# One inference step of a two-layer hybrid encoder: GpSimd's instructions in written order, weight additions issued a tile later

## The chip, the cores and the metric

The kernel runs on one core of a Trainium2 chip. TensorE multiplies, VectorE, ScalarE and GpSimd work on vectors, and DMA engines move data between HBM and the on-chip memory; a DMA is started by an instruction in the stream of SyncE (SP) or of GpSimd. The metric is the time of one launch on the device in microseconds (us). A row of the profile calls TensorE PE, VectorE DVE, ScalarE ACT and GpSimd POOL.

## The reference

There are 640 tokens (512 of a prompt, 128 of eight running streams), 1024 wide, and two layers, all in float32. The first is a Mamba-2 mixer, the second a gated MLP with position mixing (gMLP).

```python
# layer 0 (Mamba-2)
proj = rms_norm(h) @ w_in                      # -> z | x | B | C | dt
x, B, C = silu(causal_dwconv(xBC, conv_prev))  # width 4
# 32 heads in 8 groups; per chunk: decay, C B^T, states
h_new = h * exp(last) + einsum(B, w_in, x)
y = y + d_skip * x
y = gated_group_rms_norm(y, z, norm_w)
h = h + y @ w_out
# layer 1 (gMLP)
u, v, z = gelu(.), layer_norm(gelu(.)), .      # of rms_norm(h) @ w_in
h = h + (u * (W_s v + b) * silu(z)) @ w_out
y = rms_norm(h)
```

## The kernel before, in words

A float32 product is made of three products of rounded parts: an operand is split into a high part H (rounded) and a low part L (the rest), and HH, LH and HL are added up in PSUM.

**The first layer** goes through eight groups of heads, `g = 0` to `7`. A group multiplies the normed input by tiles of the input weights, 128 output columns each, by `in_proj`: x0, x1, B, C, z0 and z1. Each of x0, x1, B, C goes through `conv_tile`: VectorE scales it into `xp` (L407 to L409), ScalarE makes the first tap (`acc`, L414), VectorE adds three taps (L417), ScalarE takes a tanh (L423), VectorE ends it (`xc`, L424); TensorE then transposes `xc` into `tp` (L464). GpSimd clears three columns of `xp`, copies the cache into it and copies the new cache out of it (L405, L406, L411, L412). `pair(i)` makes the outputs of two heads from the decay matrices `E`, which `mask(i)` has multiplied by `CBm`: for `i = 0` on VectorE; for `i = 1` one `E` is masked on VectorE and one on GpSimd (both on GpSimd in the last group). `old_states` has GpSimd multiply eight slices of the old state `h0` by their decay (L582). `out_proj` multiplies the gated output of the group before by two tiles of output weights in ten pieces.

In groups 1 to 6 the written order between z0 and z1 is: `Wo = [stream.next(), stream.next()]`, `some(0, 1)`, `old_states` and other pieces, `some(1, 2)`, `some(2, 5)`, `mask(0)`, `pair(0)`, `mask(1)`, `some(5, 10)`, `pair(1)`, `gate(0)`, then z1 (a further `stream.next()`). `some(a, b)` are pieces a to b-1 of `out_proj` with `Wo`.

**Weights of the first layer** come through `Stream`, one unit for each tile. A unit has a tile `wh` and a tile `wl`; there are four buffers of each. For each unit `wsplit` writes three steps: GpSimd starts a DMA of the weights into `wh`, rounded on the way (L97); ScalarE writes their negative into `wl` (L98); GpSimd starts a second DMA of the same weights that adds into `wl` (L99). `next()` asks for units up to three behind the one that it returns, so the last unit asked for takes the buffer of the one used before the returned one. The list of units ends with sixteen of `wBv`; the second layer fetches `wBv` by itself (`v_fetch`, `v_split`, L808 to L816) and takes none of these from the stream.

**Order.** In the first layer only TensorE's instructions run as written. For every other engine a planner sets the order before the launch: it goes through a model of the time and gives an engine what is ready there. Each engine then runs its own list strictly in that order, and an instruction that waits holds up everything behind it on its engine. In the second layer all engines run as written.

**The second layer** splits its weights without GpSimd: `Forms.split` has ScalarE round a half tile (L743) and VectorE take the rest (L744). `forms.next(a)` returns a form and sees to it that `a` more behind it are split. `prod` asks for five ahead. `out_weights()` takes four forms by `forms.next(3)`; ten `out_piece` follow, each ended by a sum on VectorE (`accB`, L960).

Of the kernel before, what the change touches and what calls it, by code (L numbers as in the profile page):

```python
# [8 lines left out]
F32 = mybir.dt.float32  # L9
F32R = mybir.dt.float32r  # L10
I32 = mybir.dt.int32
AF = mybir.ActivationFunctionType
ALU = mybir.AluOpType
PSUM = bass.MemoryType.PSUM

P = 128
# [24 lines left out]
def hybrid_step(ctx: ExitStack, tc: tile.TileContext, xin, xT0, cst, wdt, cache, wA, wAo, h0in, wB, wBv, wBo,  # L41
                lnwb, spc, bsp, nwb, y_out, nconv_out, sspP_out, sspS_out, v_out):
    nc = tc.nc
    V, S, G, T = nc.vector, nc.scalar, nc.gpsimd, nc.tensor
# [46 lines left out]

    def wsplit(src):
        H = wpool.tile([P, 1024], F32R, name="wh", tag="wh", bufs=4)
        L = wpool.tile([P, 1024], F32R, name="wl", tag="wl", bufs=4)
        G.dma_start(out=H, in_=src)  # L97
        S.activation(L, H.bitcast(F32), AF.Identity, scale=-1.0)  # L98
        G.dma_start(out=L, in_=src, accum_op=ALU.add)  # L99
        return H, L  # L100

    class Stream:
        def __init__(self, srcs, ahead):
            self.srcs, self.ahead, self.got, self.n = srcs, ahead, [], 0

        def fill(self, ahead):
            while len(self.got) < min(len(self.srcs), self.n + ahead):
                i = len(self.got)
                self.got.append(wsplit(*self.srcs[i]))


        def first(self, n, between):
# [12 lines left out]

        def next(self, ahead=None):
            self.fill(1 + (self.ahead if ahead is None else ahead))
            r = self.got[self.n]
            self.got[self.n] = None
            self.n += 1  # L130
            return r
# [8 lines left out]
    def norm_first(zp, rb):  # L140
# [12 lines left out]
        for k in range(KD):  # L153
            w = C("nw0")[:, k:k + 1]
            S.activation(xH[:, k, :], xt[:, k, :], AF.Identity, scale=w)
            V.scalar_tensor_tensor(xL[:, k, :], xt[:, k, :], w, xH[:, k, :].bitcast(F32), ALU.mult, ALU.subtract)
        stream.fill(1)
        warm = ps_op.tile([P, 512], F32, name="warm", tag="op")
        for _ in range(13):
            mm(warm[:, :P], ones, ones)  # L160
# [148 lines left out]
        names += [p[0] for p in part]  # L309
        units += [p[1:] for p in part]  # L310
    units += wo(GROUPS - 2) + wo(GROUPS - 1)
    units += [(wBv[i],) for i in range(16)]
    stream = Stream(units, 3)


    with ExitStack() as ca:
# [9 lines left out]
        ptds = []  # L326
        side.append(lambda: ptds.append(norm_fin()))
        side += [lambda h=h: norm_half(*h) for h in HALVES]
        px1 = in_proj(stream.next(), xT, ps_op, "op", at=(2, 10, 12))
        ptd = ptds[0]  # L330
        nc.sync.dma_start(out=csb[1], in_=cst[:, NCST1:])

# [69 lines left out]
        def conv_tile(o0, o1, ft, j, cch, nconv):  # L402
            xp = w1.tile([P, 667], F32, name="xp", tag="xp")
            xps = xp[:, 515:667].rearrange("p (b j) -> p b j", j=19)
            G.memset(xp[:, 0:3], 0.0)  # L405
            G.tensor_copy(out=xps[:, :, 0:3], in_=cch[:, j])  # L406
            V.tensor_tensor(out=xp[:, 3:387], in0=o0, in1=rb[:, 0:384], op=ALU.mult)  # L407
            V.tensor_tensor(out=xp[:, 387:515], in0=o1[:, 0:128], in1=rb[:, 384:512], op=ALU.mult)
            V.tensor_tensor(out=xps[:, :, 3:19], in0=o1[:, 128:256].rearrange("p (b j) -> p b j", j=16),  # L409
                            in1=rb[:, 512:640].rearrange("p (b j) -> p b j", j=16), op=ALU.mult)  # L410
            G.tensor_copy(out=nconv[:, j, 0, :], in_=xp[:, 512:515])  # L411
            G.tensor_copy(out=nconv[:, j, 1:9, :], in_=xps[:, :, 16:19])  # L412
            acc = w1.tile([P, 667], F32, name="acc", tag="acc")
            S.activation(acc[:, 0:664], xp[:, 0:664], AF.Identity, scale=cw[:, 4 * ft:4 * ft + 1],  # L414
                         bias=cw[:, 128 + ft:129 + ft])
            for k in range(1, 4):
                V.scalar_tensor_tensor(acc[:, 0:664], xp[:, k:k + 664], cw[:, 4 * ft + k:4 * ft + k + 1], acc[:, 0:664],  # L417
                                       ALU.mult, ALU.add)
            xc = w1.tile([P, NT], F32, name="xc", tag="xc", bufs=5)
            accs = acc[:, 515:667].rearrange("p (b j) -> p b j", j=19)[:, :, 0:16]  # L420
            xcs = xc[:, 512:].rearrange("p (b j) -> p b j", j=16)
            for o, a in ((xc[:, :512], acc[:, :512]), (xcs, accs)):
                S.activation(o, a, AF.Tanh)  # L423
                V.scalar_tensor_tensor(o, o, 1.0, a, ALU.add, ALU.mult)  # L424
            return xc

        cio = conv_io(0)
        pB = in_proj(stream.next(), xT, ps_y, "y")
        xcs = [conv_tile(*o, ft, j, *cio) for j, (o, ft) in enumerate(((px0, 0), (px1, 1), (pB, 16)))]
        side += [cum_sums] + [lambda h=h: by_heads(*h) for h in HALVES]  # L430
        pC = in_proj(stream.next(), xT, at=(2, 9, 11))
# [351 lines left out]
    with ExitStack() as cb_:  # L783
# [162 lines left out]
        def then(n=1):  # L946
            for _ in range(min(n, len(later))):
                later.popleft()()
# [11 lines left out]
            V.scalar_tensor_tensor(h1[:, t, dsl], ps, 0.5, h1[:, t, dsl], ALU.mult, ALU.add)  # L960

        def out_weights():
            w = [forms.next(3) for _ in range(4)]
            return w[:2], w[2:]

        def out_piece(Ws, ys, p, after=None):
# [14 lines left out]
        for g in range(GROUPS):  # L981
# [9 lines left out]
            for i in range(2):  # L991
                f = 2 * g + i
                if i and 0 < g < GROUPS - 1:
                    Ws = out_weights()
                    for p in range(2 * TT):
                        out_piece(Ws, groups[g - 1], p)
                        then()
                uu = wk.tile([P, NT], F32, name="uu", tag="uu", bufs=2)
                zz = wk.tile([P, NT], F32, name="zz", tag="zz", bufs=1)
                pa, pb = (ps_m.tile([P, 512], F32, name="pqa", tag="m")[:, :HT],  # L1000
# [206 lines left out]
```

## Time and profile before

| what | value |
|---|---|
| time of three runs | 1184.87, 1185.45, 1282.32 us (median 1185.45) |
| the profiled execution | 1181.53 us, of it 1179.4 us from the first to the last instruction (span) |
| mean granted TensorE clock | 0.960 of full speed |
| busy share of the span | PE 89%, DVE 70%, ACT 38%, POOL 19% |
| instructions | 16944 |

The durations below are those of the profiled execution; what lies around its span is 2.1 us. The first layer ends and the second begins at about 680 us. A row of the timeline gives start, duration, engine, line, operation, what is written and read, how many such instructions were merged, and in brackets how long the engine had been idle before it and what ended that.

### The profile page before, as it was taken

To read this page: it belongs to the slowest core of one execution; us is meant where nothing else is said; L and a number is where in the kernel's file an instruction comes from. 1 tells how busy PE (TensorE), PEld (TensorE's weight loads), DVE (VectorE), ACT (ScalarE), POOL (GpSimd) and SP (SyncE) were. 2 spreads that over 40 slices of the span, in tenths; PEclk is the share of its full clock that TensorE was granted. 3 is DMA by queue.
4 is the path that set the end of the run, shared out by engine and by line. 5 is a ranking of instruction groups with operands and counts; after the bars stand their busy time and mean duration, and the time that the engine had idled before them with its cause. 6 is when DMAs were issued, how large, how long until landed. Compare 5 with 4: busy or idle time off the path is not lost.

```text
span 1179.4 us, 16944 instructions
## 1 busy us (share of the span) xinstructions
PE 1053.0 (89%) x6387; PEld 945.2 (80%) x6387; DVE 826.2 (70%) x1533; ACT 447.1 (38%) x804; POOL 228.2 (19%) x412
## 2 busy tenths in 40 slices
PE   7998998798889889987978949998899999999996
PEld 6987797697688678786977738887889889888985
DVE  4767866656747646756666766656788888788886
ACT  6354425244144153152252234334534333324343
POOL 3243413313314214224134100000000000000000
PEclk8898999999999989999998969998999999999998
DMA  9497676675575585676756642221124224223222
GB/s 321 108 247 196 142 200 155 137 231 135 121 232 126 132 230 136 144 200 145 207 143 155 213 115 72 72 81 50 52 81 129 67 70 125 82 82 97 84 63 89
DMA packets 66865, 161.08 MB, mean 137 GB/s; under 512 B 10176, under 2 KB 28864, under 8 KB 66784
## 3 DMA queue, kind: packets, MB, share of 16 engines
q0 software_dynamic: 19008, 69.21, 25.6%
q1 hardware_dynamic: 47776, 90.78, 24.6%
q8 instruction: 51, 0.84, 0.3%
q14 instruction: 30, 0.25, 0.1%
HBM read 143.11 MB, written 16.86 MB: 136 GB/s over the span
## 4 chain that ended last, share of the span: by engine, by line
PE 29%; DVE 22%; DMA 19%; issue 16%; ACT 8%; POOL 5%; SPq 0%; POOLq 0%; ACTq 0%; DVEq 0%
PE pv L69 9%; DMA wh<-wAo 7%; PE pop L69 6%; PE pin L69 5%; DMA wh<-wA 4%; DVE wf L744 4%; DMA dhl<-hl 3%; PE pqb L69 2%; DMA E<-laD 2%; ACT wl L98 2%; PE pqc L69 2%; DMA out_sspS<-h 2%; POOL wl L99 2%; DVE h L960 2%; PE pqa L69 1%
## 5 line engine op out<-in xcount | busy, mean ns | idle before, releaser
L69 PE MATMUL pin<-xH,wh 128*128 128x384 f32 (+1 forms) x768 | 252.5, 329 | 0.1
L69 PE MATMUL pin<-xL,wh 128*128 128x384 f32 (+1 forms) x768 | 241.8, 315 | 0.0
L69 PE MATMUL pin<-xH,wl 128*128 128x384 f32 (+1 forms) x768 | 241.7, 315 | 0.0
L69 PEld LDWEIGHTS pin<-xH,wh 128*128 128x128 f32 x768 | 149.8, 195 | 7.9 <-issue 4.3
L69 PEld LDWEIGHTS pin<-xL,wh 128*128 128x128 f32 x768 | 149.9, 195 | 0.2
L69 PEld LDWEIGHTS pin<-xH,wl 128*128 128x128 f32 x768 | 149.1, 194 | 0.0
L98 ACT ACTIVATE wl<-wh 128x1024 fp32r<-128x1024 f32 x66 | 69.9, 1059 | 192.0 <-DMA wh<-wA 102.2
L69 PE MATMUL pop<-wh,yHL 128*128 128x512 f32 x320 | 105.8, 412 | 22.8 <-DVE hs L561 13.1
L69 PE MATMUL pop<-wf,yHL 128*128 128x512 f32 x480 | 116.3, 398 | 8.7 <-DVE h L960 8.1
L417 DVE SCALAR_TENSOR_TENSOR acc<-xp,cw,acc 128x664 f32<-128x664 f32 x96 | 91.9, 957 | 35.1 <-ACT acc L414 33.5
L69 PEld LDWEIGHTS pop<-wf,yHL 128*128 128x128 f32 x480 | 88.8, 188 | 34.2 <-DVE h L960 12.8
L743 ACT CAST wf<-raw 128x512 fp32r<-128x512 f32 x128 | 76.7, 617 | 78.7 <-PE pop L69 28.8
L744 DVE TENSOR_TENSOR wf<-raw,wf 128x512 fp32r<-128x512 f32 x128 | 87.9, 692 | 25.0 <-ACT wf L743 22.6
L69 PEld LDWEIGHTS pop<-wh,yHL 128*128 128x128 f32 x320 | 58.6, 192 | 40.3 <-DVE hs L561 15.7
L424 DVE SCALAR_TENSOR_TENSOR xc<-xc,acc 128x512 f32<-128x512 f32 x64 | 35.5, 594 | 59.4 <-ACT xc L423 59.3
L99 POOL DMA_DIRECT2D wl<-wA x47 | 41.3, 878 | 176.6 <-ACT wl L98 151.5
L681 DVE SCALAR_TENSOR_TENSOR h<-pop,rr,h 128x512 f32<-128x512 f32 x80 | 59.3, 745 | 12.2 <-PE pop L69 12.1
L69 PE MATMUL pqa<-xH,wf 128*128 128x320 f32 x256 | 64.3, 320 | 3.2 <-ACT v L836 3.2
L69 PE MATMUL pqb<-tf,wf 128*128 128x320 f32 x384 | 64.1, 316 | 2.5 <-DVE zz L1022 2.5
L69 PE MATMUL pv<-wh,xL 128*128 128x512 f32 x160 | 63.4, 396 | 1.0 <-DVE xL L227 1.0
L69 PE MATMUL pop<-wl,yHL 128*128 128x512 f32 x160 | 64.0, 400 | 0.0
L69 PE MATMUL pv<-wh,xH 128*128 128x512 f32 x160 | 63.8, 398 | 0.0
(225 smaller groups left out, 2051.6 us busy)
## 6 DMA issues: line engine op xcount, KB each, us to landing
wh<-wA POOLq DMA_DIRECT2D x47, 512.0 KB, 6.6
wl<-wA POOLq DMA_DIRECT2D x47, 512.0 KB, 6.5
raw<-wB SPq DMA_DIRECT2D x32, 512.0 KB, 3.9
E<-laD SPq DMA_DIRECT2D x32, 320.0 KB, 6.5
h<-h0in SPq DMA_DIRECT2D x16, 512.0 KB, 5.2
out_sspS<-h SPq DMA_DIRECT2D x16, 512.0 KB, 6.6
wh<-wAo POOLq DMA_DIRECT2D x16, 512.0 KB, 5.8
wl<-wAo POOLq DMA_DIRECT2D x16, 512.0 KB, 5.6
```

The lines of the kernel that those rows point to most:

```text
L69: T.matmul(out, lhsT=lhsT, rhs=rhs, start=start, stop=stop, **kw)
L98: S.activation(L, H.bitcast(F32), AF.Identity, scale=-1.0)
L99: G.dma_start(out=L, in_=src, accum_op=ALU.add)
L417: V.scalar_tensor_tensor(acc[:, 0:664], xp[:, k:k + 664], cw[:, 4 * ft + k:4 * ft + k + 1], acc[:, 0:664], ALU.mult, ALU.add)
L424: V.scalar_tensor_tensor(o, o, 1.0, a, ALU.add, ALU.mult)
L681: V.scalar_tensor_tensor(h1[:, t, dsl], ps, rg[:, t:t + 1], h1[:, t, dsl], ALU.mult, ALU.add)
L743: S.copy(out=t[:, 0], in_=src)
L744: V.tensor_tensor(out=t[:, 1], in0=src, in1=t[:, 0].bitcast(F32), op=ALU.subtract)
L960: V.scalar_tensor_tensor(h1[:, t, dsl], ps, 0.5, h1[:, t, dsl], ALU.mult, ALU.add)
```

## The change

- GpSimd joins TensorE in running as written, in the first layer too.
- `Stream.fill` writes for a new unit only the DMA into `wh`. The negative copy and the adding DMA of that unit are written (`low`) just ahead of the next unit's DMA, so one tile later. Two early calls ask for fewer units ahead (`next(1)`, `next(2)`).
- The sixteen units of `wBv` are gone from the list of units.
- In `conv_tile` the clearing goes to VectorE and the three small copies to ScalarE.
- In the second layer `out_weights()` asks for no form ahead; between the ten pieces `forms.fill` splits up to four more.

```diff
-    def wsplit(src):
-        H = wpool.tile([P, 1024], F32R, name="wh", tag="wh", bufs=4)
-        L = wpool.tile([P, 1024], F32R, name="wl", tag="wl", bufs=4)
-        G.dma_start(out=H, in_=src)
-        S.activation(L, H.bitcast(F32), AF.Identity, scale=-1.0)
-        G.dma_start(out=L, in_=src, accum_op=ALU.add)
-        return H, L
...
+        def low(self):
+            if self.half:
+                H, L, src = self.half
+                S.activation(L, H.bitcast(F32), AF.Identity, scale=-1.0)
+                G.dma_start(out=L, in_=src, accum_op=ALU.add)
+                self.half = None
 
         def fill(self, ahead):
             while len(self.got) < min(len(self.srcs), self.n + ahead):
-                i = len(self.got)
-                self.got.append(wsplit(*self.srcs[i]))
+                self.low()
+                src, = self.srcs[len(self.got)]
+                H = wpool.tile([P, 1024], F32R, name="wh", tag="wh", bufs=4)
+                L = wpool.tile([P, 1024], F32R, name="wl", tag="wl", bufs=4)
+                G.dma_start(out=H, in_=src)
+                self.half = H, L, src
+                self.got.append((H, L))
...
             self.fill(1 + (self.ahead if ahead is None else ahead))
+            if len(self.got) == len(self.srcs):
+                self.low()
...
         stream.fill(1)
+        stream.low()
...
-    units += [(wBv[i],) for i in range(16)]
...
-        px1 = in_proj(stream.next(), xT, ps_op, "op", at=(2, 10, 12))
+        px1 = in_proj(stream.next(1), xT, ps_op, "op", at=(2, 10, 12))
...
-            G.memset(xp[:, 0:3], 0.0)
-            G.tensor_copy(out=xps[:, :, 0:3], in_=cch[:, j])
+            V.memset(xp[:, 0:3], 0.0)
+            S.copy(out=xps[:, :, 0:3], in_=cch[:, j])
...
-            G.tensor_copy(out=nconv[:, j, 0, :], in_=xp[:, 512:515])
-            G.tensor_copy(out=nconv[:, j, 1:9, :], in_=xps[:, :, 16:19])
...
+            S.copy(out=nconv[:, j, 0, :], in_=xp[:, 512:515])
+            S.copy(out=nconv[:, j, 1:9, :], in_=xps[:, :, 16:19])
...
-        pB = in_proj(stream.next(), xT, ps_y, "y")
+        pB = in_proj(stream.next(2), xT, ps_y, "y")
...
-            w = [forms.next(3) for _ in range(4)]
+            w = [forms.next(0) for _ in range(4)]
...
                         out_piece(Ws, groups[g - 1], p)
                         then()
+                        if p:
+                            forms.fill(min(p // 2 + 1, 4))
...
-    with _tile.TileContext(nc) as tc, tc.manual_schedule(engines={_mybir.EngineType.PE}):
+    with _tile.TileContext(nc) as tc, tc.manual_schedule(engines={_mybir.EngineType.PE, _mybir.EngineType.Pool}):
```

## Rows read from the trace of the kernel before

**Rows 1.** The page, busy time, share of the span and instructions of TensorE.
```profile
PE 1053.0 (89%) x6387; PEld 945.2 (80%) x6387; DVE 826.2 (70%) x1533; ACT 447.1 (38%) x804; POOL 228.2 (19%) x412
```
**Rows 2.** Waits of TensorE, whole span: total us, times, longest us.
```profile
PE tp L464 <- DVE xc L424: 33.9, 14, 4.9
PE pt L224 <- issue: 14.4, 1, 14.4
PE pop L69 <- DVE hs L561: 13.1, 6, 2.3
PE pop L69 <- DVE h L960: 8.1, 6, 1.3
```
**Rows 3.** Timeline of GpSimd in group 3, 379 to 406 us.
```profile
379.49 0.89 POOL L97 DMA_DIRECT2D wh<-wA  x1
381.02 4.90 POOL L582 TENSOR_TENSOR h<-h,etot 128x256 f32<-128x256 f32 x8 [0.64 <-PE yq L69]
389.78 0.88 POOL L99 DMA_DIRECT2D wl<-wA  x1 [3.86 <-ACT wl L98]
390.55 1.69 POOL L626 TENSOR_TENSOR E<-E,CBm 128x640 f32<-128x640 f32 x1
405.20 1.26 POOL L97 DMA_DIRECT2D wh<-wA  x2 [12.97 <-PE pop L69]
```
**Rows 4.** Timeline of TensorE around the end of the ten pieces, group 3.
```profile
404.89 0.62 PE L69 MATMUL pop<-wh,yHL 128*128 128x512 f32 x2
...
406.56 0.44 PE L69 MATMUL yB<-E,xdt 128*64 128x128 f32 x4
```
**Rows 5.** Timeline of VectorE, masks on both engines, group 3.
```profile
390.70 2.23 DVE L626 TENSOR_TENSOR E<-E,CBm 128x640 f32<-128x640 f32 x1
...
393.84 0.81 DVE L626 TENSOR_TENSOR E<-E,CBm 128x640 f32<-128x640 f32 x1
```
**Rows 6.** Timeline of ScalarE, then of TensorE, around one wait for `xc`.
```profile
350.88 1.06 ACT L98 ACTIVATE wl<-wh 128x1024 fp32r<-128x1024 f32 x1 [3.00 <-issue]
351.85 0.81 ACT L423 ACTIVATE xc<-acc 128x512 f32<-128x512 f32 x2
...
353.24 0.78 PE L464 MATMUL tp<-csb,xc 128*128 128x128 f32 x4 [4.11 <-DVE xc L424]
```
**Rows 7.** Window, its length, busy PE, PEld, DVE, ACT, POOL; then PEclk, DMA share, GB/s.
```profile
353.70:357.00 3.30, 3.30 (x12) 3.30 (x11) 2.70 (x14) 3.27 (x9) 0.46 (x3) 0.50 1.00 155
```
**Rows 8.** Timeline between the layers: ScalarE, VectorE, TensorE.
```profile
680.27 1.06 ACT L98 ACTIVATE wl<-wh 128x1024 fp32r<-128x1024 f32 x1 [7.76 <-DMA wh<-wBv]
...
682.82 1.22 DVE L816 TENSOR_TENSOR wl<-raw,wh 128x1024 fp32r<-128x1024 f32 x1 [7.88 <-DMA wl<-wBv]
...
692.65 1.94 PE L224 MATMUL pt<-csb,xs 128*128 128x128 f32 x8 [14.42 <-issue]
```
**Rows 9.** Timeline of VectorE, then of TensorE, at ten pieces of the second layer.
```profile
911.70 0.95 DVE L744 TENSOR_TENSOR wf<-s,wf 128x512 fp32r<-128x512 f32 x1
912.58 0.68 DVE L960 SCALAR_TENSOR_TENSOR h<-pop,h 128x512 f32<-128x512 f32 x1
...
918.51 0.73 PE L69 MATMUL pop<-wf,yHL 128*128 128x512 f32 x2 [1.35 <-DVE h L960]
```
**Rows 10.** Timeline of GpSimd, then of TensorE, at the start.
```profile
22.55 0.90 POOL L99 DMA_DIRECT2D wl<-wA  x1 [3.24 <-ACT wl L98]
...
28.39 0.83 PE L69 MATMUL pms<-ones,sqa 128*128 128x1 f32 x6 [1.96 <-DVE sqa L185]
```
**Rows 11.** Lines of GpSimd by form, first layer; then one small operation of ScalarE.
```profile
L406 POOL COPY xp<-cch 128x24 f32<-128x24 f32 x32 | 9.6, 302 | 0.0
...
52.35 0.23 ACT L383 ACTIVATE elt<-la 128x32 f32<-128x32 f32 x1
```
**Rows 12.** Timeline of GpSimd in group 7, where VectorE works beside it.
```profile
636.41 0.89 POOL L99 DMA_DIRECT2D wl<-wAo  x1 [3.97 <-ACT wl L98]
637.03 2.64 POOL L582 TENSOR_TENSOR h<-h,etot 128x256 f32<-128x256 f32 x3
```

More of the change, by code (lines that the diff above doesn't have):

```diff
@@ L90, in rsqrt @@
         return r
-    def wsplit(src):
-        H = wpool.tile([P, 1024], F32R, name="wh", tag="wh", bufs=4)
-        L = wpool.tile([P, 1024], F32R, name="wl", tag="wl", bufs=4)
-        G.dma_start(out=H, in_=src)
-        S.activation(L, H.bitcast(F32), AF.Identity, scale=-1.0)
-        G.dma_start(out=L, in_=src, accum_op=ALU.add)
-        return H, L
     class Stream:
         def __init__(self, srcs, ahead):
-            self.srcs, self.ahead, self.got, self.n = srcs, ahead, [], 0
+            self.srcs, self.ahead, self.got, self.n, self.half = srcs, ahead, [], 0, None
+        def low(self):
[4 more added lines that the diff above has]
+                self.half = None
         def fill(self, ahead):
             while len(self.got) < min(len(self.srcs), self.n + ahead):
-                i = len(self.got)
-                self.got.append(wsplit(*self.srcs[i]))
+                self.low()
[5 more added lines that the diff above has]
+                self.got.append((H, L))
         def first(self, n, between):
```

## The prediction, made before the result was known

> **What bounds the kernel now.** I read the busy shares first. TensorE is busy for 1053.0 of 1179.4 us [rows 1], no other engine comes near, and TensorE runs as written in both kernels. So a change gains only where it fills one of TensorE's idle stretches, some 126 us in all, and loses only where it opens a new one. The list of TensorE's waits came next, to learn whom it waits for: VectorE's `xc` (33.9 us, 14 times), one 14.4 us hole before `pt`, VectorE's `hs` (13.1 us) and `h` at L960 (8.1 us) [rows 2]. No weight DMA is in that list: the prefetch of the weights is hidden already. Then I went to the timelines of the other engines at each of these holes, and last through GpSimd's written order, to see what would stand behind what.
>
> **Part 1: GpSimd as written, the two output units.** This is the largest term. In groups 1 to 6 `next()` is called twice in a row for `Wo`. With three units ahead and four buffers, the second call asks for a unit whose buffer is that of the first `Wo` tile, which all ten pieces read. Its DMA can't start before the tenth piece has read that tile. In the trace of before this is seen: both such DMAs start at 405.20, after 12.97 us of waiting for TensorE's `pop` [rows 3]. The planner had put GpSimd's eight multiplications of the old state (381.02, 4.90 us) and its mask (390.55, 1.69 us) ahead of that wait [rows 3]. In written order both come behind it, for `old_states` and `mask(1)` are written after the two calls. That a GpSimd instruction waiting to issue a DMA holds up arithmetic behind it is seen in group 7: three multiplications begin only at 637.03, after an adding DMA that had waited 3.97 us for ScalarE [rows 12].
>
> Who waits for the mask: `pair(1)`, which TensorE reaches right after the tenth piece. In before its products with `E` start at 406.56 [rows 4]. After: the DMA issues from 405.20 for about 0.63 us (half of 1.26 for two), then 4.90 us, then 1.69 us [rows 3], so the mask ends at 412.4. TensorE gets through the first half of the products with `E` to 406.8, so it stands for 5.6 us. Nothing covers this: z1 is written behind `pair(1)`. Six groups make 33.6 us.
>
> The clock adds to it. After a wait of 4.11 us [rows 6] the granted clock was 0.50, that is 1.2 of 2.4 GHz, through a stretch of 3.30 us in which TensorE was busy throughout [rows 7]; half of that, 1.65 us, is lost. I take one such stretch behind each new hole: 6 x 1.65 = 9.9 us. Bounds: none, and twice as much. **Term: +43.5 us** (33.6 to 53.4). SyncE's DMAs are not moved, and none waits for this mask before `pair(1)` has run.
>
> **Part 2: the mask leaves VectorE's way.** VectorE's first mask took 2.23 us where its next took 0.81; GpSimd's ran from 390.55 to 392.24, beside it [rows 3, 5]. TensorE then waited for `hs`, which VectorE makes right after [rows 2]: six times, 2.3 us at the longest. With GpSimd's mask gone from there, 2.23 - 0.81 = 1.42 us comes off a wait. I count five groups, leaving one for a wait that was shorter: **-7 us**; bounds -5 and -12 (some clock comes back with it).
>
> **Part 3: no units of `wBv`.** Three of them were fetched at the end of the first layer, for nobody. ScalarE stood 7.76 us for the `wh` of the third, up to 680.27, with the second layer's split and norm behind it in its list; VectorE stood 7.88 us up to 682.82 for the same `wl`; TensorE had nothing from 678.2 (692.65 - 14.42) to 692.65 [rows 8]. Without them the split waits only for its own data, and the norm of the first tokens, of which `h` has been done for long, can run beside the last pieces. What is late next is VectorE: its last sums, the small steps of two norms and the low part of the transposed tile. I leave 1 to 4 us of the 14.4 us hole, and the clock can gain a little: **-14 us**, bounds -10 and -17.
>
> **Part 4: forms between the pieces.** Six times TensorE waits 1.35 us at the seventh piece for the sum of an earlier one [rows 2, 9]; that sum stood behind two splits, of which the later took 0.95 us and ended where the sum began, at 912.58 [rows 9]. Two splits are at least 1.6 us, more than the wait. They now come behind the third and fifth pieces; a sum is 0.68 us [rows 9], and a piece is six products of which two take 0.62 us [rows 4], so VectorE has room beside the pieces. **-7 us**, bounds 0 (another form is then late) and -8.1.
>
> **Part 5: the start.** GpSimd's sums of squares stood behind an adding DMA that waited 3.24 us for ScalarE, and TensorE then waited 1.96 us for the last sum [rows 10]; both adding DMAs are now written behind the sums. The first calls also fetch less beside the first input. Against it, B and C now get their low parts only a few us before use. **-2 us**, bounds -5 and +4.
>
> **Part 6: small copies.** GpSimd spent 0.30 us on a copy of the cache [rows 11]; its removal gives nothing by itself, since GpSimd is busy for 19%. The trace shows no such copy on ScalarE; the nearest row is its operation on 128x32, 0.23 us [rows 11]. Three for each of 32 tiles are 22 us on an engine that is busy for 38%. Two of them stand between `acc` and tanh, where VectorE's three taps cover them. In the 14 places where TensorE waits for `xc`, at most 0.46 us can get in: 0 to +6 us. VectorE's clearing is another 0.1 us, written ahead of a wait for TensorE. **+2 us.**
>
> **Part 7: additions a tile later.** A unit asked for three tiles ahead now gets its adding DMA one tile later, two tiles ahead of its use; `wh` and `wl` are not on the list of waits, so I cost it at **0**. If that cover were gone, a DMA's landing would show as a wait for `wl`.
>
> **Sum:** 43.5 - 7 - 14 - 7 - 2 + 2 = +15.5 us. On the profiled execution's own 1181.53 us that is 1197.0. The median of the runs is 3.9 us above the profiled one, so a median could read 1201; I keep **1197 us**, 1.0% above 1185.45. The ends of the terms, taken as independent, make about 13 us: 1184 to 1211 for this case alone.
>
> **Rivals.**
> - *ScalarE's copies stop blocking the convolution* (faster). At 350.88 ScalarE had stood 3.00 us for the landing of a weight DMA, and the tanh of the convolution came behind it; TensorE waited 4.11 us for that `xc` [rows 6]. The copy into `wl` is now written one tile later. For it: where two instructions are ready at once the planner may take the earlier written. Against it: the planner places what is ready in its model, however late it is written, and the copy is ready there when it was before. If the copies went behind, up to 33.9 us of waits [rows 2] and some five slow stretches of 1.65 us would go, 42 us; two thirds of it, 28 us, makes 1169; all of it 1155.
> - *The wait at `Wo` isn't paid* (the change doesn't do what it says there): the DMA's wait lets GpSimd's later instructions pass, or these end up ahead of it. Then part 1 goes, and part 2 with it: 1197 - 43.5 + 7 = 1160.5. Against it: rows 12.
> - *GpSimd and VectorE hold each other up in the new place* (slower). Behind the tenth piece VectorE is summing pieces and gating. Beside a busy VectorE GpSimd's three multiplications took 2.64 us [rows 12], 0.88 each, against 4.90 / 8 = 0.61 in a quiet stretch [rows 3]; with the mask at VectorE's 2.23, GpSimd needs 8 x 0.27 + 0.54 = 2.7 us more, and VectorE's own work slips by as much as 1 us: 6 x 3.7 = 22 us, 1219. It decides if GpSimd's stretch grows beyond some 9 us a group. The Trainium skill, page "SBUF — State Buffer", section "Who interferes with whom", gives such a lock as a rule: a VectorE instruction with two SBUF inputs and a GpSimd instruction that reads SBUF shut each other out for the whole instruction. By that rule the trace agrees in the masks (2.23 against 0.81).
>
> **How the numbers follow.** Chances: the forecast 0.62, copies behind 0.12, wait not paid 0.11, slower rival 0.15. A measurement of this kernel can tell about 2% from no change: below 1161.7 is faster, above 1209.2 slower. Faster: half of the second case and 0.6 of the third, 0.13. Slower: 0.13 of the last case and 0.06 from the upper end of the forecast, 0.19. The rest, 0.68, is within 2%. The range of 8 in 10 takes in the wait not paid and part of the slower rival: 1160 to 1216.
>
> **What would show it.** Right: in groups 1 to 6 a wait of TensorE for `E` from GpSimd of 5 to 6 us at `pair(1)`, with the eight multiplications and the mask behind the start of the weight DMA; VectorE's first mask at 0.8 us; the hole before `pt` below 5 us; no wait for `h` at L960; no `wBv` from GpSimd. Wrong: no such wait for `E` (part 1 falls, and the time is near 1160); waits for `xc` well below or above 33.9 us (the order on ScalarE changed); waits for `wh` or `wl` (part 7 falls).

## The result, and the profile after

The changed kernel takes 1216.27 us (median of 4 runs, 1213.09 to 1219.83), the kernel before 1185.16 in the same comparison: ratio 1.0279, 95% interval 1.0229 to 1.0328. One execution of the kernel before, 1282.32 us, fell in a slower state and is left out of the ratio. The change costs some 33 us; 1197 us was forecast, with 1216 as the upper end of the range, and the median lies 0.3 us above that. The profiled execution took 1213.09 us, its span is 1211.3.

The page of the changed kernel, the line that answers to [rows 1]:

```profile
PE 1061.1 (88%) x6387; PEld 950.9 (79%) x6387; DVE 838.5 (69%) x1565; ACT 451.7 (37%) x897; POOL 200.0 (17%) x278
```

TensorE's idle time is the span less its busy time: 150.2 us, against 126.4 before, 23.8 more. The other 8.1 us of the 31.9 that the span grew are in its busy time, for the same number of matmuls: some of them ran at the lower clock (the mean granted clock is 0.954, against 0.960).

Whom TensorE waits for in the changed kernel (in all, times, longest), as in [rows 2]:

```profile
PE yB L69 <- POOL E L633: 29.5, 6, 4.9
PE tp L471 <- DVE xc L431: 27.4, 15, 6.6
PE pin L69 <- DVE xp L416: 17.7, 5, 4.7
...
PE st L69 <- DVE h L668: 9.1, 1, 9.1
PE pop L69 <- DVE y L654: 4.7, 1, 4.7
PE pop L69 <- DVE hs L568: 4.6, 5, 0.9
...
PE pt L232 <- issue: 1.7, 1, 1.7
```

The forecast is in here: six waits for `E` from GpSimd, the hole before `pt` down from 14.4 to 1.7 us, `hs` from 13.1 to 4.6, and `h` at L960 (now L967) from 8.1 to 0.7. What was not forecast are three new lines: `xp` (17.7), `h` at L668 (9.1) and `y` at L654 (4.7), 31.5 us together. None of them names a weight or a DMA; the one wait for a weight, for `wl`, is 1.4 us.

GpSimd's timeline in group 3 of the changed kernel (start, us, then the instruction; the bracket is the idle time before it and what ended it):

```profile
341.02 0.55 POOL L112 DMA_DIRECT2D wh<-wA  x1 [11.59 <-PE pop L69]
341.58 4.60 POOL L589 TENSOR_TENSOR h<-h,etot 128x256 f32<-128x256 f32 x8
346.15 1.52 POOL L633 TENSOR_TENSOR E<-E,CBm 128x640 f32<-128x640 f32 x1
350.50 0.91 POOL L103 DMA_DIRECT2D wl<-wA  x1 [2.83 <-ACT wl L102]
351.09 0.88 POOL L112 DMA_DIRECT2D wh<-wA  x1
360.41 0.87 POOL L103 DMA_DIRECT2D wl<-wA  x1 [8.44 <-ACT wl L102]
360.97 0.86 POOL L112 DMA_DIRECT2D wh<-wA  x1
373.99 0.88 POOL L103 DMA_DIRECT2D wl<-wA  x1 [12.16 <-ACT wl L102]
374.55 0.88 POOL L112 DMA_DIRECT2D wh<-wA  x1
```

The first three lines are part 1 of the prediction as it was put: load, multiplications, mask, and `pair(1)` behind them. The rest is what the prediction never looked at. Each load (L112) is issued right behind the adding transfer of the unit before (L103); that one waits for ScalarE's copy of its unit; and the copy waits until that unit has landed. So a load can only start when the one before it has landed and been copied: a **ring**, one unit every 10 to 14 us here, whatever buffers are free. Before, two loads went out back to back at this place [rows 3].

How the ring reaches TensorE, from ScalarE's, VectorE's and TensorE's timelines of the changed kernel:

```profile
372.50 1.06 ACT L102 ACTIVATE wl<-wh 128x1024 fp32r<-128x1024 f32 x1 [8.95 <-DMA wh<-wA]
373.47 0.72 ACT L682 ACTIVATE y<-y 128x640 f32<-128x640 f32 x1
...
374.22 0.82 DVE L719 TENSOR_TENSOR y<-y 128x640 f32<-128x640 f32 x1 [9.28 <-ACT y L682]
374.96 0.28 DVE L415 TENSOR_TENSOR xp<-pin,rb 128x128 f32<-128x128 f32 x1
375.16 0.28 DVE L416 TENSOR_TENSOR xp<-pin,rb 128x128 f32<-128x128 f32 x1
...
375.59 0.55 PE L69 MATMUL pin<-xH,wh 128*128 128x256 f32 x1 [4.66 <-DVE xp L416]
```

To be read from the bottom up: TensorE waits until VectorE has written `xp`, since that frees the PSUM bank of `pin`; `xp` stands in VectorE's list behind a sum that waits for a square; the square stands in ScalarE's list behind the copy of a weight unit; the copy stands 8.95 us for a landing. ScalarE and VectorE run in the order that the planner made for them, and neither goes past what it waits for. So a late weight load shows up as a wait for the convolution. The three new lines hold six waits of more than 3 us (four for `xp`, one for `h`, one for `y`), 29.2 of the 31.5 us. Before each of them ScalarE's list has such a copy, and right behind it the step for which VectorE stood. The four copies ahead of the waits for `xp` stood 7.68, 8.95, 7.69 and 8.13 us for their landings, and those ahead of the waits for `h` and `y`:

```profile
98.68 1.06 ACT L102 ACTIVATE wl<-wh 128x1024 fp32r<-128x1024 f32 x1 [8.73 <-DMA wh<-wA]
...
701.51 1.06 ACT L102 ACTIVATE wl<-wh 128x1024 fp32r<-128x1024 f32 x1 [7.44 <-DMA wh<-wAo]
```

### The profile page after: what moved, and what is told of

The parts are those of the page before. It is cut to its first block, busy times and chain, and to the rows that moved or that the text cites. A ratio compares the mean times of both kernels' runs of the same rounds, so it can differ in the third digit from the quotient of the medians.

```text
span 1211.3 us, 16913 instructions
## 1 busy us (share of the span) xinstructions
PE 1061.1 (88%) x6387; PEld 950.9 (79%) x6387; DVE 838.5 (69%) x1565; ACT 451.7 (37%) x897; POOL 200.0 (17%) x278
## 4 chain that ended last, share of the span: by engine, by line
PE 29%; issue 23%; DVE 18%; DMA 14%; POOL 8%; ACT 7%; SPq 0%; POOLq 0%; ACTq 0%; DVEq 0%
PE pv L69 8%; PE pop L69 8%; DMA wh<-wA 4%; DMA wh<-wAo 4%; PE pqb L69 3%; DMA dhl<-hl 3%; POOL h L589 3%; DVE wf L751 3%; PE pin L69 2%; PE pqc L69 2%; PE pqa L69 2%; POOL wl L103 2%; POOL wh L112 2%; DVE acc L424 2%; DVE h L967 1%
## 5 line engine op out<-in xcount | busy, mean ns | idle before, releaser
L69 PE MATMUL pin<-xH,wh 128*128 128x384 f32 (+1 forms) x768 | 256.6, 334 | 22.2 <-DVE xp L416 17.7
L69 PE MATMUL pin<-xH,wl 128*128 128x384 f32 (+1 forms) x768 | 244.8, 319 | 1.4 <-DMA wl<-wA 1.4
L69 PE MATMUL pin<-xL,wh 128*128 128x384 f32 (+1 forms) x768 | 245.0, 319 | 0.0
L69 PEld LDWEIGHTS pin<-xH,wh 128*128 128x128 f32 x768 | 153.1, 199 | 32.4 <-issue 24.4
L102 ACT ACTIVATE wl<-wh 128x1024 fp32r<-128x1024 f32 x63 | 66.5, 1056 | 264.6 <-DMA wh<-wA 142.8
L69 PEld LDWEIGHTS pin<-xH,wl 128*128 128x128 f32 x768 | 152.3, 198 | 2.0 <-DMA wl<-wA 2.0
L69 PEld LDWEIGHTS pin<-xL,wh 128*128 128x128 f32 x768 | 153.5, 200 | 0.2
L424 DVE SCALAR_TENSOR_TENSOR acc<-xp,cw,acc 128x664 f32<-128x664 f32 x96 | 91.8, 956 | 37.6 <-ACT acc L419 36.1
L103 POOL DMA_DIRECT2D wl<-wA x47 | 41.5, 883 | 348.4 <-ACT wl L102 315.7
L431 DVE SCALAR_TENSOR_TENSOR xc<-xc,acc 128x512 f32<-128x512 f32 x64 | 28.7, 489 | 61.0 <-ACT xc L430 60.8
L69 PE MATMUL pv<-wl,xH 128*128 128x512 f32 x160 | 63.1, 395 | 0.0
```

What stands on the lines that cost most here:

```text
L69: T.matmul(out, lhsT=lhsT, rhs=rhs, start=start, stop=stop, **kw)
```

## The experiments

All ratios are to the kernel before, measured beside each kernel on the same chip; two kernels that were measured at different times are compared by these ratios. Line numbers are those of the changed kernel, in runs 4 and 10 those of the kernel before. ScalarE's and VectorE's lists are made anew by the planner for every kernel, so an edit of one line can also move instructions there.

**1. The wait at `Wo` taken away.** The second call finds its unit already requested, so no load stands ahead of the multiplications (of `hv`, a part of the old state) and the mask.

```
-                Wo = [stream.next(), stream.next()]
+                Wo = [stream.next(), stream.next(2)]
```

> The changed kernel, but the second output-projection unit of a group is taken with two units ahead, so that GpSimd has no transfer that waits for the pieces ahead of hv and the E mask. Theory (the wait at Wo costs the six yB steps, 28.7 us of idle TensorE and some 9 us of clock; the other 31 us over the forecast come from a ring in the weight transfers): the yB waits fall from 29.5 us to below 5 us, the waits for xp, h at L668 and y at L654 stay (17.7, 9.1 and 4.7 us within some us), contention of mask and scans comes back for at most 7 us, time 1180 to 1190 us. Rival A (what stands behind the late xp is the same wait at Wo, which pushes everything after it): the xp waits fall as well, time about 1165 us. Rival B (the wait only moves to the next transfer of the group): the wait comes back elsewhere, time above 1205 us.

Measured: 1205.01 us, ratio 1.0203 [1.0167, 1.0238], 0.8% or 9 us below the changed kernel's ratio. TensorE's waits:

```profile
PE tp L471 <- DVE xc L431: 50.3, 19, 7.5
PE pin L69 <- DVE xp L414: 14.8, 7, 2.7
PE pop L69 <- DVE hs L568: 12.4, 6, 2.3
...
PE st L69 <- DVE h L668: 7.3, 1, 7.3
PE pop L69 <- DVE y L654: 4.9, 1, 4.9
```

The waits for GpSimd's `E` are gone, and those for `xc` grew from 27.4 to 50.3 us, those for `hs` from 4.6 to 12.4. My expectation of 1180 to 1190 missed. The trace fits this reading: TensorE comes to the next tile sooner and finds it just as late. This is rival B in its effect, at its border of 1205, but through another engine: not another transfer of GpSimd's holds TensorE, but VectorE's `xc`. What made `xc` late, this run alone doesn't tell.

**2. The ring opened.** On top of 1, `fill` issues the next load ahead of the adding transfer of the unit before.

```
-                self.low()
                 src, = self.srcs[len(self.got)]
...
                 G.dma_start(out=H, in_=src)
+                self.low()
```

> As the run before, and in fill the plain load of the next unit is issued ahead of the adding transfer of the unit before it, so that the load no longer stands behind an adding transfer that waits for ScalarE's copy. Theory (ring of transfers): loads go out some 8 us earlier, ScalarE's copy L102 no longer holds its engine for the landing, the waits for xp (17.7 us), h at L668 (9.1 us) and y at L654 (4.7 us) shrink to below half together, time 15 to 30 us below the run before, 1155 to 1170 us. Rival (the small copies, now on ScalarE and VectorE, make xp late): these waits stay, and the time is that of the run before within 5 us. Rival (an adding transfer that now stands behind a load waiting for a free buffer comes too late): TensorE waits for wl, time above the run before.

Measured: 1115.9 us, ratio 0.9439 [0.9408, 0.9469]: 7.6% of the time of before, some 90 us, below run 1, for one line moved. The page, and what is left of the waits:

```profile
PE 1039.4 (93%) x6387; PEld 938.8 (84%) x6387; DVE 815.8 (73%) x1565; ACT 455.4 (41%) x897; POOL 206.2 (19%) x278
```

```profile
PE tp L471 <- DVE xc L431: 30.7, 7, 6.0
PE pop L69 <- DVE hs L568: 4.8, 6, 0.9
```

TensorE's idle time fell from 138.2 us in run 1 to 74.6, and its busy time by 22.5 us for the same matmuls (mean granted clock 0.953, then 0.972). The waits for `h` at L668 and for `xp` at L416 are gone, and `y` at L654 is at 0.9 us. The copy and the adding transfers, first in the changed kernel (busy, mean ns; idle before and what ended it):

```profile
L102 ACT ACTIVATE wl<-wh 128x1024 fp32r<-128x1024 f32 x63 | 66.5, 1056 | 264.6 <-DMA wh<-wA 142.8 <-issue 66.5 <-DMA wh<-wAo 25.3
...
L103 POOL DMA_DIRECT2D wl<-wA x47 | 41.5, 883 | 348.4 <-ACT wl L102 315.7 <-DVE u L360 9.3 <-ACT nconv L421 9.3
```

then with the load first:

```profile
L102 ACT ACTIVATE wl<-wh 128x1024 fp32r<-128x1024 f32 x63 | 66.5, 1056 | 116.4 <-DMA wh<-wA 85.6 <-DMA wh<-wAo 17.5 <-PE pin L69 4.9
...
L103 POOL DMA_DIRECT2D wl<-wA x47 | 41.8, 890 | 78.0 <-ACT wl L102 69.9 <-DVE rs L200 5.6 <-ACT E L517 0.4
...
L111 POOL DMA_DIRECT2D wh<-wA x47 | 29.0, 618 | 201.5 <-PE pin L69 132.3 <-PE pop L69 68.3 <-POOLq L1198 0.8
```

Ahead of the adding transfers GpSimd waits far less for ScalarE's copy (315.7 us down to 69.9); with the loads it now waits for TensorE to free a buffer (132.3 us by `pin`, 68.3 by `pop`): at these the prefetch is as deep as its buffers allow. ScalarE's idle time ahead of its copies falls from 264.6 to 116.4 us. The theory's direction held, its size did not: I had taken the ring to cost the three new waits, 15 to 30 us; opening it gave three times that.

**3. GpSimd back to the planner**, the rest of the change kept.

```
-    ... tc.manual_schedule(engines={_mybir.EngineType.PE, _mybir.EngineType.Pool}):
+    ... tc.manual_schedule(engines={_mybir.EngineType.PE}):
```

> The changed kernel, with GpSimd's order left to the planner as before; all the rest of the change stays. Theory (written order alone makes both the wait at Wo and the ring): no yB wait above 5 us, xp, h and y waits back to the size before, forms and start gains kept (14 + 7 + 2 us), time about 1160 us (1155 to 1168). Rival (small copies make xp late): no yB wait, xp waits stay at some 15 us, time about 1172 us. Rival (the additions a tile later are a loss in any order, because the program hands them to the planner late): ScalarE still waits for landings at L102 and time is 1180 us or more.

Measured: 1163.65 us, ratio 0.9846 [0.9819, 0.9872], as the theory had it. TensorE's list has no wait for GpSimd's `E`, and 0.7 us for `xp` at L416. So the whole loss, and more, comes with the written order: 1.0279 - 0.9846 = 0.0433, 51 us, while the rest of the change gains 18 us.

**4. The written order alone**, in the kernel before: adding transfer right behind its load, small copies on GpSimd.

```
-    ... tc.manual_schedule(engines={_mybir.EngineType.PE}):
+    ... tc.manual_schedule(engines={_mybir.EngineType.PE, _mybir.EngineType.Pool}):
```

> The kernel before, with GpSimd in written order and nothing else: each adding transfer right behind its plain load, small copies on GpSimd as before, wBv units and forms as before. Theory (an adding transfer ahead of the next load makes the ring, and here GpSimd also waits out its own unit's landing and ScalarE's copy before it may compute): slower than before by 40 to 100 us, 1225 to 1285 us, GpSimd waiting some 600 us for ScalarE's copy. Rival (it is the delay of the addition by a tile that costs, not the order): within 15 us of 1185 us.

Measured: 1275.67 us, ratio 1.0815 [1.0769, 1.0861]: +94 us, inside the theory's range. The wait for `E` doubles:

```profile
PE yB L69 <- POOL E L626: 62.8, 6, 10.6
```

The theory's own number for GpSimd's waits for the copy, some 600 us, was too high: they are 380.4 us. (ScalarE's idle time ahead of its copies is 274.3 us.) Here no addition is delayed, and the loss is greater, so it doesn't need the delay by a tile. So written order is far dearer by itself (94 us) than within the changed kernel (51 us): other parts of the change give back some 43 us of it. Parts 5 to 7 are the likely ones; runs 11 and 12 show a gain from two of them, though in another kernel.

**5. Load first, `Wo` as in the change.** Against the changed kernel only:

```
-                self.low()
                 src, = self.srcs[len(self.got)]
...
                 G.dma_start(out=H, in_=src)
+                self.low()
```

> The changed kernel with one thing changed: in fill the plain load of the next unit is issued ahead of the adding transfer of the unit before it. The second output-projection unit is asked for as in the change. Theory (two losses that add: the ring of transfers, 89 us between the two runs before, and the load at Wo that stands ahead of hv and the E mask, 11 us between the changed kernel and the first run): 1120 to 1130 us, with yB waits of 10 us or more. Rival (with the ring gone, the load at Wo costs its whole 29.5 us and the clock behind it): 1145 to 1155 us. Rival (the order of load and adding transfer only pays together with the change at Wo): 1190 us or more.

Measured: 1139.61 us, ratio 0.9641 [0.9578, 0.9705], between the theory and its first rival.

```profile
PE yB L69 <- POOL E L633: 35.0, 6, 5.8
```

With runs 1 and 2 this makes a square: taking away the wait at `Wo` gives 0.8% with the ring and 2.0% (24 us) without it; opening the ring gives 6.4% with that wait and 7.6% without it. The two losses overlap: each hides part of the other, though the 1.3% by which the two differ is hardly wider than the intervals allow. That the gain of opening the ring comes from the planner's new lists instead is unlikely here: 879 of ScalarE's 897 instructions, 59 of the 63 copies among them, and 1444 of VectorE's 1565 stand in the same order as in the changed kernel. For VectorE's remaining ones it isn't excluded.

**6. Load first, order by the planner.** Against the kernel of run 2:

```
-    ... tc.manual_schedule(engines={_mybir.EngineType.PE, _mybir.EngineType.Pool}):
+    ... tc.manual_schedule(engines={_mybir.EngineType.PE}):
```

> The kernel with the load ahead of the adding transfer and two units ahead at Wo (1116 us), with GpSimd's order left to the planner. Theory (a load that stands behind an adding transfer goes out late in either way of ordering, and the planner keeps the program's order of the two where it sees no reason against): 1115 to 1135 us, GpSimd's waits for ScalarE's copy well below 100 us. Rival (the planner puts the adding transfer first by its own due times, so that the program's order decides nothing): 1160 to 1166 us, as with the change's order under the planner. The run then also says that the written order of GpSimd is what the gain needs.

Measured: 1160.34 us, ratio 0.9828 [0.9779, 0.9878]: the rival. The two runs with the planner differ by 0.2%, less than their intervals. GpSimd waits for the copies about as long in either:

```profile
L103 POOL DMA_DIRECT2D wl<-wA x47 | 41.3, 878 | 239.9 <-ACT wl L102 232.4 <-ACT Bt L473 6.7 <-DMA stk<-dhl 0.8
```

(In run 3 the idle time is 244.3 us.) The kernel before has such waits too, 176.6 us ahead of its `wl<-wA`, 151.5 of them for the copy. The planner didn't find the order of run 2, even from a program in which the load stands first; in this kernel it took the written order to have it.

**7. The copy moved from ScalarE to GpSimd** in the changed kernel, to see whether the loss passes through ScalarE's list.

```
-                S.activation(L, H.bitcast(F32), AF.Identity, scale=-1.0)
+                G.tensor_scalar(out=L, in0=H.bitcast(F32), scalar1=-1.0, scalar2=None, op0=ALU.mult)
```

> The changed kernel with the negated copy of each weight unit made by GpSimd, which waits for the landing anyway, in place of ScalarE. Loads go out as late as in the changed kernel or later. If the loss comes through ScalarE's list, which stands at the copy until the landing while squares, convolution and norms stand behind it: TensorE's waits for xp, h at L668 and y at L654 (17.7, 9.1, 4.7 us) fall below 10 us together, and the time falls to 1150 to 1195 us, less what the slower copy on GpSimd gives back. If the loss is that units themselves reach TensorE late: the time stays at 1216 us or rises, with TensorE waiting for wh or wl. If GpSimd's copy disturbs VectorE: VectorE's instructions beside it get longer, and the time rises above 1216 us.

Measured: 1255.15 us, ratio 1.0635 [1.0586, 1.0684].

```profile
L102 POOL TENSOR_SCALAR wl<-wh 128x1024 fp32r<-128x1024 f32 x63 | 179.7, 2853 | 343.9 <-issue 165.5 <-PE pin L69 85.8 <-DMA wh<-wA 21.8
```

```profile
PE pop L69 <- DMA wl<-wAo: 34.6, 7, 6.8
...
PE pin L69 <- DVE xp L416: 24.0, 6, 4.4
```

The copy takes 2.85 us there against 1.06 on ScalarE, and makes the ring longer: now TensorE waits for the units themselves, as the second case had it. The third case is in it too: VectorE's L424 takes 1.09 us in the mean, against 0.96. The waits for `h` at L668 (4.3 us) and `y` at L654 (0.9) shrink, those for `xp` grow. This settles nothing about ScalarE: its list was relieved, but the ring got worse at the same time.

**8. Part 3 alone** in the kernel before: no `wBv` units.

```
-    units += [(wBv[i],) for i in range(16)]
```

> The kernel before without the 16 wBv units at the end of the weight stream (part 3 of the change alone). Forecast of the prediction: the 14.4 us hole at pt goes, -14 us, 1168 us. Rival (something else stands right behind the hole): -3 us or less.

Measured: 1168.63 us, ratio 0.9899 [0.9865, 0.9934], -12 us, inside the bounds. Most of the hole's 14.4 us was to be had.

**9. Part 4 alone** in the kernel before: loads and forms between the pieces.

```
-            w = [forms.next(3) for _ in range(4)]
+            w = [forms.next(0) for _ in range(4)]
...
+                        if p:
+                            forms.fill(min(p // 2 + 1, 4))
```

> The kernel before with the loads of the gMLP's output weights and their forms placed between the pieces of the projection (part 4 alone). Forecast: six waits for h at L960 (8.1 us) go, -7 us, 1175 us. Rival (the split work on VectorE only moves to where the pieces need it): 0, 1182 us.

Measured: 1174.01 us, ratio 0.9941 [0.9919, 0.9963], -7 us as forecast.

**10. Part 6 alone** in the kernel before: the zeroing on VectorE, the three small copies on ScalarE.

```
-            G.memset(xp[:, 0:3], 0.0)
-            G.tensor_copy(out=xps[:, :, 0:3], in_=cch[:, j])
+            V.memset(xp[:, 0:3], 0.0)
+            S.copy(out=xps[:, :, 0:3], in_=cch[:, j])
...
-            G.tensor_copy(out=nconv[:, j, 0, :], in_=xp[:, 512:515])
-            G.tensor_copy(out=nconv[:, j, 1:9, :], in_=xps[:, :, 16:19])
...
+            S.copy(out=nconv[:, j, 0, :], in_=xp[:, 512:515])
+            S.copy(out=nconv[:, j, 1:9, :], in_=xps[:, :, 16:19])
```

> The kernel before, with the convolution's zeroing on VectorE and its three small copies on ScalarE, as in the change, and nothing else. Theory (ring; copies nearly free): 0 to +6 us, 1185 to 1191 us, TensorE's waits for xp below 5 us in all. Rival (the copies are what makes xp late in the changed kernel): +10 to +15 us, with xp waits of TensorE of some 15 us. Rival (copies on GpSimd had blocked the convolution, so moving them gains): 1155 to 1170 us.

Measured: 1179.98 us, ratio 0.9993 [0.9969, 1.0017]: no difference. TensorE waits 0.7 us for `xp` at L409, which is L416 of the changed kernel, and once 3.4 us for the clearing at L405. So the moved copies by themselves are not what makes `xp` late; this is shown for the planner's order of GpSimd only.

**11. Part 5 taken back** in the fast kernel of run 2.

```
         stream.fill(1)
-        stream.low()
...
-        px1 = in_proj(stream.next(1), xT, ps_op, "op", at=(2, 10, 12))
+        px1 = in_proj(stream.next(), xT, ps_op, "op", at=(2, 10, 12))
...
-        pB = in_proj(stream.next(2), xT, ps_y, "y")
+        pB = in_proj(stream.next(), xT, ps_y, "y")
```

> The fast kernel (load ahead of the adding transfer, two units ahead at Wo, 1116 us) with the units at the start asked for as in the kernel before (part 5 of the change taken back). Theory (fetching fewer units ahead leaves the input's transfers the room, some 7 us earlier at 97 us in the changed kernel, and with the load first the low parts are in time): slower by 4 to 10 us, 1120 to 1126 us. Rival (at the start the change brings nothing by itself): within 3 us of 1116 us.

Measured: 1127.97 us, ratio 0.9562 [0.952, 0.9604], 1.2% or 15 us slower than run 2: more than expected. A wait for a weight's addition shows:

```profile
PE pin L69 <- DMA wl<-wA: 5.5, 1, 5.5
```

**12. Part 6 taken back** in the fast kernel: zeroing and small copies on GpSimd again, the last two still behind `acc`.

```
-            V.memset(xp[:, 0:3], 0.0)
-            S.copy(out=xps[:, :, 0:3], in_=cch[:, j])
+            G.memset(xp[:, 0:3], 0.0)
+            G.tensor_copy(out=xps[:, :, 0:3], in_=cch[:, j])
...
-            S.copy(out=nconv[:, j, 0, :], in_=xp[:, 512:515])
-            S.copy(out=nconv[:, j, 1:9, :], in_=xps[:, :, 16:19])
+            G.tensor_copy(out=nconv[:, j, 0, :], in_=xp[:, 512:515])
+            G.tensor_copy(out=nconv[:, j, 1:9, :], in_=xps[:, :, 16:19])
```

> The fast kernel (1116 us) with the convolution's zeroing and three small copies back on GpSimd, still in written order (part 6 taken back). Theory (in written order the copies stand behind loads that wait for a buffer, and xp stands behind the copies): the convolution waits for GpSimd, TensorE's waits for xp or xc grow, slower by 15 to 60 us, 1130 to 1175 us. Rival (there is room for them between the transfers): within 6 us of 1116 us.

Measured: 1142.26 us, ratio 0.9666 [0.9611, 0.9721], 2.3% or 27 us slower than run 2, inside the theory's range. In written order, then, it matters where these copies run. TensorE's waits for `xc` come 18 times where there were 7, though with 24.7 us in all against 30.7; waits for `hs` are 11.4 us against 4.8. By which way the 27 us arise, these rows don't settle: the profiled execution of this kernel was 8 us faster than its median.

Run 2 is the fastest of all these kernels, the kernel before and the changed one included.

## Why the prediction was wrong

The direction was right and the wait at `Wo` came as described; the step that failed is **Part 7: "`wh` and `wl` are not on the list of waits, so I cost it at 0"**, and with it the sentence that carried it, "the prefetch of the weights is hidden already". With nothing changed but the load ahead of the adding transfer, the changed kernel is 6.4%, some 76 us, faster (run 5). The place that I named for a check, a wait of TensorE for `wl`, stayed nearly empty (1.4 us), and yet the order of the weight transfers was the largest cost that any run took out of the changed kernel. By the trace they act on ScalarE, which must copy each unit, and from there on work that has nothing to do with weights. I asked of the adding transfer only who uses its result, and not what is issued behind it on GpSimd: the next load. It was in the trace of before that an adding transfer had stood 3.97 us for ScalarE with arithmetic behind it [rows 12]. The 76 us are not the size of the miss, which is 19 us: opening the ring brings the kernel to 1139.61 us, far below the forecast, because the kernel before has a good part of these waits too (run 6), and I had taken them for hidden. Nor does the loss need the delay by a tile, which part 7 is named for: with each addition right behind its load the written order costs still more (run 4).

Shown by runs: moving the load ahead of the adding transfer gives 76 and 90 us (run 5 against the changed kernel, run 2 against run 1), and only with GpSimd as written (run 6). Read from the trace only: that the loss passes through ScalarE's list; run 7, meant to separate this, did not. The timeline at 372.50 to 375.59 shows it for one wait and the other copies named there for the others. The longest is that for `h` at L668, late behind a convolution step at 99.65 that stood behind the copy at 98.68:

```profile
99.65 0.93 ACT L419 ACTIVATE acc<-xp,cw 128x664 f32<-128x664 f32 x1
...
105.34 1.39 PE L69 MATMUL st<-stk 64*128 64x256 f32 x4 [9.09 <-DVE h L668]
```

Point by point:

- **Part 1** (+43.5): the waits are 29.5 us against 33.6. The list in [rows 2] had left out that TensorE waited at this same place before, for VectorE's own mask; of these 7.9 us 1.6 are left:

```profile
PE yB L69 <- DVE E L626: 7.9, 4, 3.7
```

  The multiplications and the mask took 4.60 and 1.52 us, against 4.90 and 1.69 in [rows 3]. The clock behind a hole is as in [rows 7], 0.50; in the changed kernel, one window after the hole that ends at 347.73 (length, busy PE, PEld, DVE, ACT, POOL, then PEclk):

```profile
348.10:351.50 3.40, 3.40 (x23) 3.07 (x20) 1.60 (x4) 1.68 (x2) 1.00 (x2) 0.50 0.00 0
```

  But its price as a term of a sum was wrong. Removing the wait gave 9 us with the ring in place and 24 us without. A wait that is seen is not what its removal returns, when another late thing stands behind it.
- **Part 2** (-7): `hs` from 13.1 to 4.6 us, 8.5; VectorE's mask takes 0.81 to 0.83 us in 22 of 23 places, as forecast.
- **Part 3** (-14): 12.7 us less at `pt`, -12 us in run 8. **Part 4** (-7): 7.4 us less at `h`, -7 us in run 9.
- **Part 5** (-2): at the end of the start it had gained a little (the first `st` at 76.05 us against 77.50), and then 9.1 us went at a later `st`, at 105.34; the aside "B and C now get their low parts only a few us before use" had looked for the loss at B's and C's own `wl`, not on ScalarE. Without the ring part 5 is worth 15 us (run 11).
- **Part 6** (+2): 0 by run 10, but only where the planner orders GpSimd. I priced it on the old order; in written order it is worth 27 us (run 12).
- **The sum**: parts 3 to 6 were put at -21 us, and the change without the written order measured -18. The written order with the mask was put at +36.5 us and measured +51. These 15 us and 3 us make 18 of the miss of 19; the rest is that 1197 stands on the profiled execution's 1181.53 us. In TensorE's terms: the waits were put at +5.6 us in sum (43.5 without its 9.9 of clock, and the other parts), and its idle time grew by 23.8; the clock was put at 9.9, and busy time grew by 8.1. So the miss lies in waits, and the three new lines (31.5 us) are larger than it; shorter waits for `xc` (6.5 us less) and for VectorE's mask (6.3) made up for part. That the forecast missed by no more than 19 us is in part luck.
- **Rivals**: the third, GpSimd and VectorE holding each other up, gave 1219 and so the nearest time, and its mechanism is there, but turned round. GpSimd's stretch was 6.7 us a group (341.02 to 347.67), below the 9 from which it was to decide, and TensorE's wait at most 4.9 us; it was VectorE that was held, by some 5 us in each of six groups where 1 us at most had been allowed for, as the last section shows. No run shows what this costs by itself. The first rival, copies of ScalarE that stop blocking the convolution, had the right place with the wrong sign: they block it longer (264.6 us of ScalarE's idle time end at a copy, against 192.0 before; for landings of `wA` 142.8 against 102.2). What it hoped to gain at most was 42 us.

## What to carry to other kernels

When an engine that issues transfers gets its instructions in a fixed order, follow each transfer that waits for another engine, and ask what is issued behind it: if that is the next load of the same stream, the loads run one at a time, and here moving the load one place forward opened this. A list of waits without weights doesn't mean that the weights are hidden: see who converts or copies them, how long that engine stands for a landing (a sum in the listing by line), and what is next in its list. Sum up waits as gains only if the work behind them is already done by then, and price an edit in the order in which it will run, not in the old one.

## What the runs showed of the hardware

One VectorE instruction stood for nearly all of GpSimd's multiplications and mask. Two such instructions of the changed kernel are VectorE's L302 and L679, which take 0.88 and 0.86 us in the mean of run 2:

```profile
342.27 6.09 DVE L302 SCALAR_TENSOR_TENSOR yHL<-y,csb,yHL 128x640 fp32r<-128x640 f32 x1
...
90.85 7.02 DVE L679 TENSOR_TENSOR y<-y,th 128x640 f32<-128x640 f32 x1
```

The first ends at 348.36, just after GpSimd's eight multiplications and mask (341.58 to 347.67); the second lies beside the same nine instructions in the first group. L302 is held so once in each of groups 1 to 6 (6.09 or 6.10 us each; in run 5 7.01 to 7.04). So one VectorE instruction waited out a whole series, not one instruction of it. The Trainium skill, page "SBUF — State Buffer", section "Who interferes with whom", has the two shut each other out for the whole instruction; the trace agrees, and adds that in these seven places a series without a gap counted as one. It is also where VectorE's added busy time comes from: 838.5 us, and 816.4 with the multiplications elsewhere (run 1). TensorE waits for that very mask meanwhile, but the hold also feeds the ring. The load issued at 341.02 landed 4.3 us later, at 345.3, and ScalarE could copy it only at 349.03, behind a square that waited for the held L302:

```profile
348.39 0.74 ACT L682 ACTIVATE y<-y 128x640 f32<-128x640 f32 x1 [6.64 <-DVE yHL L302]
349.03 1.04 ACT L102 ACTIVATE wl<-wh 128x1024 fp32r<-128x1024 f32 x1
```

Where GpSimd issues two transfers of 512 KB right behind each other (0.6 us apart in the timeline above), the one issued first landed sooner, in the median and in either order. Median us from issue to landing, in the changed kernel, with the addition first:

```profile
wh<-wA POOLq DMA_DIRECT2D x47, 512.0 KB, 7.2
wl<-wA POOLq DMA_DIRECT2D x47, 512.0 KB, 5.6
```

and in run 2, with the load first:

```profile
wh<-wA POOLq DMA_DIRECT2D x47, 512.0 KB, 5.4
wl<-wA POOLq DMA_DIRECT2D x47, 512.0 KB, 8.0
```

So the order also decides which of the two lands later, and it is the load that ScalarE waits for.
